# Strassen's step of the gate and up product starts one block earlier (block 4 instead of 5), with one token sum made by accumulating transfers

## The chip, the cores and the metric

The kernel runs on one core of a Trainium2 chip. The core has a matrix engine (TensorE, PE in the rows; PEld is its weight load), a vector engine (VectorE, DVE), a scalar engine (ScalarE, ACT), GpSimd (POOL) and SyncE (SP), each with its own instruction stream that it works off in order, and 16 DMA engines that the streams of SP, ACT and POOL feed. The metric is the device time of one execution in microseconds (us), lower is better. The kernel before takes 902.25 us (median of 3 runs, 900.49 to 902.29).

## The reference, cut to what matters

One decoder layer for 512 tokens of width 1024. After the token mixers comes the feed-forward part, and there the change lies:

```python
    h = rmsnorm(x, norm_ffn_pre[i])                       # 512 x 1024
    gate, up = jnp.split(h @ ffn_w_gate_up[i], 2, axis=-1)  # two products with 1024 x 2816
    x = x + rmsnorm((jax.nn.silu(gate) * up) @ ffn_w_down[i], norm_ffn_post[i])
```

All of it is float32. The change leaves the results the same up to rounding.

## The kernel before, in words

**The split.** Each operand of a product is cut into a rounded high part and a low rest (`h` by a ScalarE copy into the type fp32r, `l` by a VectorE subtraction `x - h`), and a product is three matmuls: high x high, high x low, low x high. The normed tokens lie transposed in `aTh` (high) and `aTl` (low), as 8 slices of 128 model channels by 512 tokens.

**The blocks.** Gate and up have 22 blocks each (`f` = 0 to 21) of 128 output channels. A block loads 512 KB of gate and 512 KB of up weights by SP (`raw` tiles), cuts them (`wh`, `wl`), and multiplies.

- Blocks 0 and 1 run ahead of the loop, blocks 2 to 4 in the ordinary form: 2 x 8 x 3 = 48 matmuls of 512 columns (`gu_mm`), then ScalarE's silu and VectorE's product (`gu_act`, the `L1192` and `L1193` rows).
- From `f == SF` on (SF = 5 before) a block runs in Strassen's form (`s_block`): gate and up weights are seen as a 2 x 2 block matrix (gate or up, lower or upper half of the model channels), the tokens as another (halves of the channels, halves of the tokens). Seven products of 12 matmuls of 256 columns replace eight. They use sums of weights, made anew for each block (`s_load`: `s12`, `s34`, then cut to `w12`, `w34`, and `vw`, whose low part is finished by an accumulating DMA from POOL, `L1325`), and sums of tokens T1 to T4, made once ahead of the first such block (`t_sums`).

**The token sums.** With lo1, lo2 the lower channels of the first and second half of the tokens and hi1, hi2 the upper ones, each in a high and a low part: T1 = lo1 - lo2, T3 = hi2 - lo2, T2 = T3 - lo1 up to sign, T4 = T2 - hi1 up to sign. Each elementary step is one VectorE instruction over 128 x 1024 elements; then the sum is cut (`cut`: ScalarE copy `L1268`, VectorE subtraction `L1269`). T4 is written over lo2 in `aTh` and `aTl`. Before, step 0 (T1) runs ahead of block 2, step 1 (T3) ahead of block 3, step 2 (T2, and the uncut T4) ahead of block 4, step 3 (the cut of T4) ahead of block 5.

**The order of the products in `s_block`.** gate-lower x lo1 into bank X (its sum is P1), gate-upper x hi1 into W, then `w12`-upper x T2 into X again, *on top of* P1; so this third product cannot begin before ScalarE has copied P1 out of X (`nc.scalar.copy(P1, X)`, `L1362`). Then `w12`-lower x T1, `w34`-lower x T3, `w34`-upper x hi2, `vw` x T4.

**What sets the order.** TensorE's order is the program's (`strict`). On the other engines a scheduler puts instructions in order at build time: DMAs and cuts of weights inside `tc.high_priority(offset=...)` are pulled ahead of what is written before them; the rest stays near the order of the text. A tile of a pool that is named again waits until its last reader is through.

**Weight buffers.** `s_raw` takes five buffers in turn: three of the ring `rawf`, and the two 512 KB tiles `x1_0` and `x1_1`, which come free early, as soon as two tiles of the residual are stored (`L1157`). `loads[0]` says at which of the five it starts.

Of the kernel before, what the change touches and what calls it, by code (L numbers as in the profile page):

```python
# [8 lines left out]
F32 = mybir.dt.float32  # L9
F32R = mybir.dt.float32r  # L10
BF16 = mybir.dt.bfloat16
AF = mybir.ActivationFunctionType
OP = mybir.AluOpType
# [21 lines left out]
TV = (12, 7, 8, 11)  # L35
VP = (4,)

SF = 5
SA = 160
WARM = 13  # L40

# [1 line left out]
def f32(ap):  # L43
    return ap.bitcast(F32)
# [3 lines left out]
def layer_kernel(ctx, tc, a, out):  # L48
    nc = tc.nc
# [13 lines left out]
    def nm(s):  # L63
        uid[0] += 1
        return f"{s}{uid[0]}"

    def bank(tag, shape=None):
        return ps.tile(shape or [128, 512], F32, tag=tag, name=nm(tag), bufs=PB[tag])
# [1054 lines left out]
    def gu_load(f, up=None):  # L1123
        return (wload(wgu[:, :, f * 128:(f + 1) * 128], [128, KT, 128], "f"),
                wload(wgu[:, :, DFF + f * 128:DFF + (f + 1) * 128], [128, KT, 128], "f", up))
# [41 lines left out]
    NJ2, HS = NF // 2, S // 2  # L1167
# [3 lines left out]
    def gu_mm(w, banks, cs, then=None):  # L1171
        for i, ((wh, wl), p_) in enumerate(zip(w, banks)):
            three(p_[:, cs], [(wh[:, k], wl[:, k], aTh[:, k, cs], aTl[:, k, cs]) for k in range(KT)],
                  {TK[2]: then} if i == 1 and then else {})

    def gu_act(f, pg, pu):

        j, odd = divmod(f, 2)
        b, jj = divmod(j, 2)
        if not odd:  # L1180
            ST[j] = ff.tile([128, 2, S], F32, tag="st" if j else "s10", name=nm("st"), bufs=2 if j else 1)
        st = ST[j][:, odd]
        if odd and jj == 0:
            n = len(BLK[b])
            RA[b] = dram.tile([128, n, 4, HS], F32, name=nm("rd"))
            A11[b] = ff.tile([128, n, 2, HS], F32R, tag=f"a{b}", name=nm("a"))
        r = ff.tile([128, 4, HS], F32, tag="rs", name=nm("r")) if odd else None
        o_ = r[:, 0:2].rearrange("p a q -> p (a q)") if odd else st
        if callable(pg):
            pg(st, o_)  # L1190
        else:
            last["silu"] = tab(nc.scalar.activation(st, pg, AF.Silu))  # L1192
            nc.vector.tensor_mul(o_, pu, st)  # L1193
        if not odd:
            return
        x = ST[j]
        e, s_ = x[:, 0], x[:, 1]
        ah = A11[b][:, jj]
        nc.scalar.copy(ah[:, 0], e[:, :HS])
        nc.vector.tensor_sub(ah[:, 1], e[:, :HS], f32(ah[:, 0]))  # L1200
        nc.vector.tensor_add(r[:, 3], e[:, HS:], r[:, 1])
        nc.vector.tensor_sub(s_[:, :HS], r[:, 3], e[:, :HS])
        nc.vector.tensor_sub(s_[:, HS:], e[:, :HS], e[:, HS:])
        nc.vector.tensor_sub(r[:, 2], r[:, 0], s_[:, :HS])
        nc.gpsimd.dma_start(RA[b][:, jj], r)
        s23 = ff.tile([128, 2, 2, HS], F32R, tag=f"s{j}", name=nm("s"))
        sv = s_.rearrange("p (o q) -> p o q", o=2)
        nc.scalar.copy(s23[:, :, 0], sv)
        nc.vector.tensor_sub(s23[:, :, 1], sv, f32(s23[:, :, 0]))
        S23[j] = s23  # L1210
# [33 lines left out]
    SB = {}  # L1244
    half = KT // 2
    tokens = [slice(0, HS), slice(HS, S)]

    def part_of(lo_hi, tok):
        ks = slice(half * lo_hi, half * lo_hi + half)
        return aTh[:, ks, tokens[tok]], aTl[:, ks, tokens[tok]]  # L1250

    def home(tag, shape, dt=F32R):
        return ff.tile(shape, dt, tag=tag, name=nm("T"))

    def t_sums(step):

        if step == 0:
            SB["tmp"] = [home(t_, [128, half, HS], F32) for t_ in ("s8", "s9")]
        n_ = ("T1", "T3", "T2", "T4")[step]
        SB[n_] = part_of(0, 1)  # L1260
        if step < 3:
            t_ = home(n_.lower(), [128, 2, half, HS])
            SB[n_] = t_[:, 0], t_[:, 1]
        x, z = SB["tmp"]
        lo1, lo2, hi1, hi2 = ([f32(v) for v in part_of(a_, b_)] for a_ in range(2) for b_ in range(2))

        def cut(n_, v):
            nc.scalar.copy(SB[n_][0], v)  # L1268
            nc.vector.tensor_sub(SB[n_][1], v, f32(SB[n_][0]))  # L1269

        def diff(o_, t_, p_, q_):
            nc.vector.tensor_sub(o_, p_[0], q_[0])
            nc.vector.tensor_sub(t_, p_[1], q_[1])
            nc.vector.tensor_add(o_, o_, t_)

        def minus(o_, v, q_):
            nc.vector.scalar_tensor_tensor(o_, v, -1.0, q_[0], op0=OP.mult, op1=OP.subtract)
            nc.vector.tensor_sub(o_, o_, q_[1])

        if step == 0:  # L1280
            diff(x, z, lo1, lo2)
            cut("T1", x)
        elif step == 1:
            diff(z, x, hi2, lo2)
            cut("T3", z)
        elif step == 2:
            minus(x, z, lo1)
            cut("T2", x)
            minus(z, x, hi1)
        else:  # L1290
            cut("T4", z)

    loads = [0]

    def s_raw(src):

# [9 lines left out]
    def s_load(f):  # L1306
# [21 lines left out]
        def behind(name):  # L1328

            if f == SF:  # L1330
                name = {"P5": "silu", "U3": "cut"}[name]
# [15 lines left out]
    def s_block(f):  # L1347
        gw, w12, w34, vw = s_load(f)
        X, Z, W = (bank(t_)[:, :HS] for t_ in ("mm", "sc", "tr"))
        if f == SF:  # L1350
            SB["tmp"] = home("tm", [128, half, HS], F32)
        P1, P5, U2, U3 = (SB["tmp"][:, i] for i in range(half))

        def times(p_, w, at, b, fresh=False):
            for k in range(half):
                for n_, (u, m_) in enumerate(((0, 0), (0, 1), (1, 0))):
                    mm(p_, w[u][:, at + k], b[m_][:, k], start=fresh and k == 0 and n_ == 0,
                       stop=k == half - 1 and n_ == 2, skip_group_check=not fresh)

        def act(st, o_):  # L1360
            times(X, gw, 0, part_of(0, 0), True)
            nc.scalar.copy(P1, X)  # L1362
            times(W, gw, half, part_of(1, 0), True)
            nc.vector.tensor_add(st[:, :HS], W, P1)
            times(X, w12, half, SB["T2"])
            nc.scalar.copy(U2, X)
            times(Z, w12, 0, SB["T1"], True)
            last["P5"] = nc.scalar.copy(P5, Z)
            times(X, w34, 0, SB["T3"])
            last["U3"] = nc.scalar.copy(U3, X)  # L1370
            times(Z, w34, half, part_of(1, 1))
            nc.vector.tensor_add(st[:, HS:], Z, U2)
            last["silu"] = tab(nc.scalar.activation(st, st, AF.Silu))
            times(X, vw, 0, SB["T4"])
            nc.vector.tensor_add(U3, U3, P5)
            nc.vector.scalar_tensor_tensor(o_[:, :HS], X, -1.0, st[:, :HS], op0=OP.mult, op1=OP.mult)
            last["o2"] = nc.vector.scalar_tensor_tensor(o_[:, HS:], U3, -1.0, st[:, HS:], op0=OP.mult, op1=OP.mult)

        gu_act(f, act, None)

    strict[0] = True
    for f in range(2, NF):
        if f - 2 <= SF - 2:
            t_sums(f - 2)
        if f >= SF:
            s_block(f)
            continue
        w, banks = gu_load(f), (bank("mm"), bank("sc"))
        gu_mm(w, banks, slice(0, S))
        gu_act(f, *banks)  # L1390
# [127 lines left out]
    for b, js in enumerate(BLK):  # L1518
# [4 lines left out]
        for jj, j in enumerate(js):  # L1523
            with tc.high_priority(offset=dn[0]):
                x = ff.tile([128, 2, 2, HS], F32R, tag=f"s{3 + j % 4}", name=nm("p"))
# [199 lines left out]
```

## Time and profile before

| what | value |
|---|---|
| runs before | 902.25 us median (900.49, 902.25, 902.29) |
| profiled execution | 901.4 us, span 899.6 us from the first to the last instruction, so 1.8 us around it |
| granted TensorE clock, mean over the span | 0.999 of full speed |
| busy: PE, PEld, DVE, ACT, POOL | 888.6, 763.2, 705.1, 556.7, 160.0 us |
| DMA moved | 110.94 MB |

The span is the time that the profile sees; sums below are made against 901.4 us, the time of that same execution, which lies 0.85 us under the median. An engine that is busy nearly all the time sets the end, if its work follows itself without gaps; of the others only those instructions matter for which it waits. Times of instructions are us from the start of the span.

### The profile page before, as it was taken

What the parts mean: (1) busy time and instruction counts of PE and PEld (TensorE: products, weight loads), DVE (VectorE), ACT (ScalarE), POOL (GpSimd) and SP (SyncE); (2) the same over time, 40 slices, a digit from 0 to 9 for tenths busy, and PEclk for the clock granted to TensorE, in tenths of its full rate; (3) what the DMA queues carried; (4) which work ended last, traced back from release to release, by engine and by line L of the source; (5) the groups of instructions that cost most, each with busy time, mean ns of one, the idle gap of its engine ahead of it and who ended that gap; (6) DMA issues with size and microseconds to landing.
All of it is one profiled execution on the core that took longest, in us unless ns stands there. A gap on an engine that the chain in (4) does not pass through costs nothing.

```text
span 899.6 us, 14169 instructions
## 1 busy us (share of the span) xinstructions
PE 888.6 (99%) x5105; PEld 763.2 (85%) x5105; DVE 705.1 (78%) x1366; ACT 556.7 (62%) x1072; POOL 160.0 (18%) x247
## 2 busy tenths in 40 slices
PE   8999999999999999999999999999999999999997
PEld 6977888878888888888888988999999988878886
DVE  6657786968788788787857588888888898888852
ACT  6468958667677667767735345766676653466520
POOL 4001201214143232323402100111111100002000
PEclk9999999999999999999999999999999999999999
DMA  9433335292114111111138244666566665658511
GB/s 300 95 94 100 111 97 162 72 163 64 45 45 106 48 48 48 47 48 47 36 133 254 94 129 118 165 164 153 142 175 168 168 217 181 195 179 243 174 58 47
DMA packets 138934, 110.94 MB, mean 123 GB/s; under 512 B 6936, under 2 KB 119664, under 8 KB 138864
## 3 DMA queue, kind: packets, MB, share of 16 engines
q1 hardware_dynamic: 126272, 95.61, 36.2%
q0 software_dynamic: 12576, 14.42, 8.2%
q8 instruction: 40, 0.66, 0.3%
q14 instruction: 30, 0.25, 0.1%
q10 hardware_dynamic: 16, 0.00, 0.0%
HBM read 97.96 MB, written 8.91 MB: 119 GB/s over the span
## 4 chain that ended last, share of the span: by engine, by line
PE 89%; DVE 5%; ACT 3%; DMA 2%; issue 1%; SPq 1%; POOL 0%; DVEq 0%; ACTq 0%
PE mm L100 46%; PE sc L100 19%; PE tr L100 7%; PE mq L100 7%; PE pv L100 5%; PE tr L103 4%; DVE wl L162 1%; DMA KS<-KS 1%; DMA y<-in_w_in_dram 1%; DVE e L845 1%; ACT e L848 1%; DVE PT L931 1%; ACT wh L161 1%; PE sc L103 0%; DVE r L644 0%
## 5 line engine op out<-in xcount | busy, mean ns | idle before, releaser
L100 PE MATMUL mm<-aTh,wh 128*128 128x512 f32 (+1 forms) x400 | 159.1, 398 | 0.1
L100 PE MATMUL mm<-aTl,wh 128*128 128x512 f32 (+1 forms) x400 | 153.3, 383 | 0.1
L100 PE MATMUL mm<-aTh,wl 128*128 128x512 f32 (+1 forms) x400 | 153.3, 383 | 0.0
L860 POOL TENSOR_SCALAR e<-e,sm 128x128 f32<-128x128 f32 (+3 forms) x128 | 77.3, 620 | 154.8 <-DVE sm L856 89.9
L162 DVE TENSOR_TENSOR wl<-raw,wh 128x1024 fp32r<-128x1024 f32 x59 | 73.1, 1242 | 28.2 <-ACT wh L161 23.6
L848 ACT ACTIVATE e<-e,mn 128x128 f32<-128x128 f32 (+3 forms) x128 | 71.5, 560 | 28.1 <-DVE mn L845 18.0
L100 PEld LDWEIGHTS mm<-aTh,wl 128*128 128x128 f32 x400 | 75.3, 188 | 15.1
L100 PEld LDWEIGHTS mm<-aTh,wh 128*128 128x128 f32 x400 | 75.4, 189 | 14.3 <-issue 3.4
L100 PEld LDWEIGHTS mm<-aTl,wh 128*128 128x128 f32 x400 | 75.6, 189 | 10.9 <-DVE aTl L248 0.5
L161 ACT CAST wh<-raw 128x1024 fp32r<-128x1024 f32 x59 | 61.6, 1048 | 28.5 <-PE mm L100 25.2
L845 DVE CUSTOM_DVE_ANT_0 e<-sc,toep 128x128 f32<-128x128 f32 (+3 forms) x128 | 59.7, 484 | 16.5 <-PE sc L100 15.5
L931 DVE TENSOR_TENSOR PT<-tr,PT 128x512 fp32r<-128x512 f32 x96 | 56.5, 595 | 15.3 <-ACT PT L930 14.7
L930 ACT CAST PT<-tr 128x512 fp32r<-128x512 f32 x96 | 47.8, 510 | 24.1 <-PE tr L103 23.2
L1316 DVE TENSOR_TENSOR w<-T,w 128x1024 fp32r<-128x1024 f32 x34 | 41.6, 1223 | 22.0 <-ACT w L1315 22.0
L100 PE MATMUL sc<-KS,QS 128*128 128x512 f32 (+2 forms) x192 | 54.3, 365 | 0.3 <-DMA KS<-KS 0.3
L100 PE MATMUL mm<-T,w 128*128 128x256 f32 x408 | 54.0, 282 | 0.0
L100 PE MATMUL mm<-aTh,w 128*128 128x256 f32 x272 | 51.5, 282 | 0.0
L100 PEld LDWEIGHTS mm<-T,w 128*128 128x128 f32 x408 | 50.9, 189 | 0.0
L103 PE MATMUL tr<-ident,e 128*128 128x128 f32 x320 | 48.6, 273 | 0.6 <-DVE PT L931 0.6
L103 PEld LDWEIGHTS tr<-ident,e 128*128 128x128 f32 x320 | 39.8, 140 | 9.6 <-DVE PT L931 0.8
L100 PEld LDWEIGHTS mm<-aTh,w 128*128 128x128 f32 x272 | 43.1, 189 | 0.0
L100 PE MATMUL mm<-T,aTh 128*128 128x512 f32 (+1 forms) x144 | 41.1, 371 | 0.0
(437 smaller groups left out, 2260.0 us busy)
## 6 DMA issues: line engine op xcount, KB each, us to landing
raw<-in_w_in_dram SPq DMA_DIRECT2D x48, 512.0 KB, 3.8
raw<-in_ffn_w_gate_up_dram SPq DMA_DIRECT2D x44, 512.0 KB, 4.1
raw<-in_ffn_w_down_dram SPq DMA_DIRECT2D x25, 512.0 KB, 4.4
rd<-r POOLq DMA_DIRECT2D x11, 512.0 KB, 4.1
w<-in_ffn_w_gate_up_dram POOLq DMA_DIRECT2D x17, 256.0 KB, 5.5
raw<-in_ple_w_gate_dram SPq DMA_DIRECT2D x8, 512.0 KB, 4.4
x<-in_x_dram SPq DMA_DIRECT2D x7, 512.0 KB, 7.9
raw<-in_w_out_dram SPq DMA_DIRECT2D x6, 512.0 KB
```

The lines of the kernel that those rows point to most:

```text
L100: return pe(nc.tensor.matmul(*args, **kw))
L103: return pe(nc.tensor.transpose(*args))
L161: nc.scalar.copy(h, RAW[n])
L162: nc.vector.tensor_sub(l, RAW[n], f32(h))
L845: nc.vector.tensor_tensor_reduce(e[:, br, :], src, toep[:, 384 - 128 * i:S], SLOPE[h], BIG, op0=OP.add, op1=OP.min, accum_out=mn[:, u, br: ...
L848: tt(nc.scalar.activation(e[:, br, :], e[:, br, :], AF.Exp, scale=-1.0, bias=mn[:, u, br:br + 1], accum_out=sm[:, u, br:br + 1]))
L860: nc.gpsimd.tensor_scalar(ev, ev, sm[:, v, br:br + 1], 1.0, op0=OP.mult, op1=OP.mult)
L930: nc.scalar.copy(P[:, 0, :2 * n], pt[:, :2 * n])
L931: nc.vector.tensor_sub(P[:, 1, :2 * n], pt[:, :2 * n], f32(P[:, 0, :2 * n]))
L1316: nc.vector.tensor_sub(l, x, f32(h))
```

## The change

The first Strassen block is block 4. All four steps of the token sums must be through one block earlier: step 0 ahead of block 2, steps 1 and 2 ahead of block 3, step 3 ahead of block 4. The three VectorE instructions of T3 go: ScalarE writes -lo2 (high part into `z`, low part into `w_`), and three accumulating DMAs from POOL add `w_`, hi2's high part and hi2's low part into `z`, 512 KB each, into the same bytes and so one after the other. Two more 512 KB tiles (the homes `s7` and `s6`) hold `z` and `w_`. The buffers start at the fourth of five (`loads = [3]`), so that block 4's gate and up weights go into `x1_0` and `x1_1`.

```diff
-SF = 5
+SF = 4
...
         if step == 0:
-            SB["tmp"] = [home(t_, [128, half, HS], F32) for t_ in ("s8", "s9")]
+            SB["tmp"] = [home(t_, [128, half, HS], F32) for t_ in ("s8", "s9", "s7", "s6")]
...
-        x, z = SB["tmp"]
+        x, y_, z, w_ = SB["tmp"]
...
         if step == 0:
-            diff(x, z, lo1, lo2)
+            nc.scalar.activation(z, lo2[0], AF.Copy, scale=-1.0)
+            nc.scalar.activation(w_, lo2[1], AF.Copy, scale=-1.0)
+            for v in (w_, *hi2):
+                nc.gpsimd.dma_start(z, v, accum_op=OP.add)
+            diff(x, y_, lo1, lo2)
             cut("T1", x)
         elif step == 1:
-            diff(z, x, hi2, lo2)
             cut("T3", z)
...
-    loads = [0]
+    loads = [3]
...
-        if f - 2 <= SF - 2:
-            t_sums(f - 2)
+        for step in {2: (0,), 3: (1, 2), SF: (3,)}.get(f, ()):
+            t_sums(step)
```

Lines behind `t_sums` carry numbers that are 4 higher after the change (`L1362` is now `L1366`, `L1315` `L1319`, `L1316` `L1320`, `L1325` `L1329`).

POOL, from the last rows ahead of the feed-forward loop on, in the kernel before (`xd`: the stored residual, `r` to `rd`: a block's values kept in DRAM, `w`: the low part of `vw`):

```order
L1157 DMA xd_5279<-x_5027 128x1024
L1157 DMA xd_5280<-x_5028 128x1024
L1205 DMA rd_5542<-r_5544 128x1024
L1205 DMA rd_5542<-r_5698 128x1024
L1325 DMA w_5806<-in_ffn_w_gate_up_dram 128x4x128
```

and the same place now (`T_5559` is `z`, `T_5560` is `w_`):

```order
L1157 DMA xd_5279<-x_5027 128x1024
L1157 DMA xd_5280<-x_5028 128x1024
L1285 DMA T_5559<-T_5560 128x1024
L1205 DMA rd_5542<-r_5544 128x1024
L1285 DMA T_5559<-aTh 128x4x256
L1285 DMA T_5559<-aTl 128x4x256
L1329 DMA w_5745<-in_ffn_w_gate_up_dram 128x4x128
```

The second accumulating transfer stands behind the store of `r`, which VectorE's `L1204` of blocks 0 and 1 must have finished; each waits for the landing of the one before it.

VectorE from the end of the ordinary block 2 on, now (`T_5557` is `x`: T2 uncut; `T_5637`, `T_5640` the cut T3 and T2; the `w` rows are low parts of weights; `raw_5853`, `raw_5855` are block 5's weights):

```order
L1200 TENSOR_TENSOR a_5543<-st_5634,a_5543 128x256
L1277 SCALAR_TENSOR_TENSOR T_5557<-T_5559,aTh 128x1024
L1269 TENSOR_TENSOR T_5637<-T_5559,T_5637 128x1024
L1278 TENSOR_TENSOR T_5557<-T_5557,aTl 128x1024
L1277 SCALAR_TENSOR_TENSOR T_5559<-T_5557,aTh 128x1024
L1320 TENSOR_TENSOR w_5738<-T_5733,w_5737 128x1024
L1269 TENSOR_TENSOR T_5640<-T_5557,T_5640 128x1024
L1341 TENSOR_TENSOR T_5862<-raw_5855 128x512
L1278 TENSOR_TENSOR T_5559<-T_5559,aTl 128x1024
L1320 TENSOR_TENSOR w_5750<-T_5734,w_5749 128x1024
```

The second of these rows is the first that reads `z` after the transfers; all rows behind it wait with it. Ahead of this piece the four weight sums of block 4 (128 x 512 each) now stand in front of the first token sum.

ScalarE around the copy of P1, before (block 5, P1's copy is `L1362`) and now (block 4, `L1366`):

```order
L1322 CAST w_5805<-raw_5787 128x512
L1323 ACTIVATE w_5806<-w_5805 128x512
L1268 CAST aTh<-T_5558 128x4x256
L1315 CAST w_5810<-T_5795 128x512 x2
L1199 CAST a_5820<-st_5780 128x256
L1362 COPY T_5818<-mm_5815 128x256
```

```order
L1326 CAST w_5744<-raw_5726 128x512
L1268 CAST T_5640<-T_5557 128x1024
L1327 ACTIVATE w_5745<-w_5744 128x512
L1319 CAST w_5749<-T_5734 128x512 x2
L1268 CAST aTh<-T_5559 128x4x256
L1366 COPY T_5757<-mm_5754 128x256
```

In both the high part of T4 (`aTh<-T`) is cut ahead of the copy of P1; now it stands directly ahead of it.

## Rows read from the trace of the kernel before

**Rows 1.** The page, part 1: busy us (share of the span) and instructions of each engine.

```profile
PE 888.6 (99%) x5105; PEld 763.2 (85%) x5105; DVE 705.1 (78%) x1366; ACT 556.7 (62%) x1072; POOL 160.0 (18%) x247
```

**Rows 2.** The chain that ended last, merged, blocks 3 to 6: start, us, what.

```profile
534.22 5.44 PE mm L100 x24
...
545.10 5.44 PE mm L100 x24
...
557.41 1.44 PE tr L100 x12
...
567.39 1.44 PE tr L100 x12
```

**Rows 3.** Who waited for whom on PE over the whole span, the longest: total, times, longest.

```profile
PE sc L100 <- DVE warm L374: 1.4, 1, 1.4
```

**Rows 4.** Timeline of PE, first matmuls of block 4 and of block 5's first three products.

```profile
544.93 0.39 PE L100 MATMUL mm<-aTh,wh 128*128 128x512 f32 x1
...
555.81 0.28 PE L100 MATMUL mm<-aTh,w 128*128 128x256 f32 x1
...
557.25 0.28 PE L100 MATMUL tr<-aTh,w 128*128 128x256 f32 x1
...
558.68 0.52 PE L100 MATMUL mm<-T,w 128*128 128x256 f32 x3
```

**Rows 5.** Timeline of ACT, blocks 2 to 5.

```profile
522.38 1.09 ACT L1192 ACTIVATE st<-mm 128x512 f32<-128x512 f32 x2
...
528.36 1.05 ACT L1268 CAST T<-T 128x1024 fp32r<-128x1024 f32 x1 [0.51 <-DVE T L1274]
...
553.29 1.05 ACT L1268 CAST aTh<-T 128x1024 fp32r<-128x1024 f32 x1
...
557.45 0.37 ACT L1362 COPY T<-mm 128x256 f32<-128x256 f32 x1 [0.21 <-PE mm L100]
```

**Rows 6.** Timeline of DVE, start of block 2.

```profile
521.11 1.23 DVE L89 TENSOR_TENSOR wl<-raw,wh 128x1024 fp32r<-128x1024 f32 x1 [1.66 <-ACT wh L88]
522.25 1.22 DVE L1272 TENSOR_TENSOR T<-aTh 128x1024 f32<-128x1024 f32 x1
...
525.12 0.68 DVE L1193 TENSOR_TENSOR r<-sc,st 128x512 f32<-128x512 f32 x1
525.72 0.41 DVE L1200 TENSOR_TENSOR a<-st,a 128x256 fp32r<-128x256 f32 x1
526.05 0.42 DVE L1201 TENSOR_TENSOR r<-st,r 128x256 f32<-128x256 f32 x1
```

**Rows 7.** Line L1205: plain stores of 512 KB from POOL, ns on POOL, landing.

```profile
L1205 POOL DMA_DIRECT2D rd<-r x11: 531/576/578, 528.9 to 729.5; - x11
...
DMA to landing us min/median/max: 2.9/4.1/4.4
```

**Rows 8.** Line L1325: accumulating transfers of 256 KB from DRAM, 512-byte pieces.

```profile
L1325 POOL DMA_DIRECT2D w<-in_ffn_w_gate_up_dram x17: 1264/1274/1364, 553.7 to 715.2; - x17
...
DMA to landing us min/median/max: 5.1/5.5/6.9
```

**Rows 9.** Line L1552: four accumulating transfers of 256 KB within SBUF, 2 KB pieces.

```profile
DMA to landing us min/median/max: 4.1/7.1/8.6
```

**Rows 10.** DMA queues, 553.6 to 560.5, one L1325: packets, MB, share of 16 engines.

```profile
q0 software_dynamic: 528, 0.26, 31.3%
```

**Rows 11.** DMA queues, 825 to 838, the four L1552.

```profile
q0 software_dynamic: 576, 1.05, 46.2%
```

**Rows 12.** Timeline of PE at the start: warming matmuls of 512 columns.

```profile
1.45 3.17 PE L100 MATMUL sc<-warm 128*128 128x512 bf16 x7 [1.45 <-DVE warm L374]
...
4.75 2.73 PE L100 MATMUL sc<-warm 128*128 128x512 bf16 x6
```

**Rows 13.** Windows at the end: length, busy PE PEld DVE ACT POOL, PEclk, DMA, GB/s.

```profile
894.00:895.00 1.00, 0.68 (x6) 0.47 (x4) 0.28 (x1) 0.00 (x0) 0.00 (x0) 1.00 0.38 131
...
898.00:899.00 1.00, 0.00 (x0) 0.00 (x0) 0.00 (x0) 0.00 (x0) 0.00 (x0) 0.60 0.00 0
```

## The prediction

> **What bounds the kernel now.** I read the page's busy shares first, then the chain that ended last, then TensorE's waits, and only then the timelines of the engines around block 4. TensorE is busy for 888.6 of 899.6 us [rows 1], and its longest wait in the whole span is 1.4 us, at the very start [rows 3]. So between blocks there is nothing to gain from making another engine faster; time is saved only by giving TensorE less to do, and lost wherever something it needs comes late. The reader should see in [rows 2] that the chain through this stage is TensorE alone, one block after another: an ordinary block takes 545.10 - 534.22 = 10.88 us, a Strassen block (from one `tr` product to the next) 567.39 - 557.41 = 9.98 us.
>
> **What the change removes.** One ordinary block becomes a Strassen block: 10.88 - 9.98 = 0.90 us. That is the whole gain. It is 0.1% of the run, and a measurement of this kernel can tell about 0.2% (1.8 us) from no change. The three VectorE instructions that go (1.14 us each by the distance of starts in [rows 6]) are worth nothing by themselves, since TensorE does not wait for VectorE in this stage.
>
> **What it adds to the path.** Everything block 4 needs must now be ready one block earlier. In the new order the token sum T3 comes out of a chain of three transfers, and I follow that chain.
>
> *Its start.* ScalarE's two silu copies of blocks 0 and 1 run at 522.38 and take 1.09 [rows 5]. The two negated copies come next, 128 x 1024 each; a plain copy of that size takes 1.05 [rows 5], so `w_` is ready at 522.38 + 1.09 + 2.10 = 525.6.
>
> *First transfer.* 512 KB in 4 KB pieces. A plain store of that size lands in 2.9 at the least [rows 7]; for the adding I allow 4.6 (worked out below), so 530.2. The bounds, 2.9 and 8.6, give 528.5 and 534.2.
>
> *The store behind it.* POOL's next row is `rd<-r`, and it needs VectorE's `L1204`. From the start of the third cut at 521.11, VectorE now does 1.14 for it, four weight sums at 0.60 = 2.40, one token difference 1.14, two products 1.20, four short rows at 0.33 = 1.33, another token row 1.14 (distances of starts, [rows 6]): 521.11 + 8.35 = 529.46, and `L1204`, of the same shape as `L1201`, ends 0.42 later at 529.9. POOL spends 0.58 on the store [rows 7], so the second accumulating transfer goes out at 530.45, whether the first one took 2.9 or 4.9.
>
> *Second and third transfer.* The trace has no such transfer: 512 KB, SBUF to SBUF, adding, in 512 pieces of 1 KB. The nearest row is `L1325`, also adding, also 512 pieces, but of 512 bytes: 5.1 to 6.9, median 5.5 [rows 8]. Its packets hold each of the 16 engines for 31.3% of 6.9 us = 2.16 us [rows 10]. The four transfers of 256 KB in 2 KB pieces hold them for 46.2% of 13 us, 1.50 us each [rows 11]. For 512 KB that makes 3.0 us in 2 KB pieces and 4.3 in 512-byte pieces; for 1 KB I take 3.3, which is 1.1 to 1.2 more than `L1325` holds them. So 5.5 + 1.0 = 6.5 us each. Lower bound 2.9, the fastest plain transfer of 512 KB [rows 7]; upper bound 8.6, the slowest accumulating one [rows 9]. I stay near `L1325`, because it shares the pieces' number and the POOL time (1.27 us) with the new ones. They add into the same bytes and cannot overlap: the last lands at 530.45 + 6.5 + 6.5 = 543.45.
>
> *From the landing to TensorE.* VectorE stands at the first `L1277`, the first reader of `z`: seven rows of 6.1 us in all (four of 1.14, two of 0.60, one of 0.33) lie between `L1204` and it, so it is there at about 536 to 537. From it on come, in order, six rows of 1.14 (T2's two steps, the cut of T3, T4's first step, the low part of `w12`, the cut of T2), one weight sum of 0.60 and T4's second step of 1.14: 8.58 us. Then ScalarE cuts T4 (1.05) and only then copies P1 (0.37) [rows 5]. With 0.1 for the hand-over that is 10.1 us. The third product of block 4 adds onto P1's bank, so it cannot start before that copy: 543.45 + 10.1 = 553.55.
>
> *When TensorE wants it.* Block 4 begins at 544.93, and its third product would begin 558.68 - 555.81 = 2.87 later, at 547.80 [rows 4]. The wait is 553.55 - 547.80 = 5.75 us. It covers the others: T1, T3 and the first weights are there by then, `w34` is cut 1.14 behind T4's difference and so before P1's copy, and T4's low part, five VectorE rows and some 4 us later, is wanted four products, 5.7 us, after the third one starts. Block 5's weights wait behind the same VectorE queue, but TensorE's own stall gives that back. So the wait is paid once.
>
> *What costs nothing.* The two loads into `x1_0` and `x1_1` take the place that two loads for blocks 6 and later had in SP's order, ahead of blocks 2's and 3's last loads, so they are early. The weight sums moved ahead delay the `L1193` rows of blocks 0 and 1 by 1.3 us; their bank is wanted again only half a block later. Were that cover gone, it would cost those 1.3 us.
>
> **Sum.** -0.90 + 5.75 = +4.85 us. From the profiled 901.4 that is 906.25; the median of the runs, 902.25, lies 0.85 higher, so 907.1.
>
> **A limit to keep in mind.** No wait arises if the last transfer lands by 547.80 - 10.1 = 537.7. Gain and loss cancel at 538.6 (4.1 us for each of the two transfers), and the loss passes 0.2% at 540.4 (5.0 us each). The whole question is on which side of 4.1 to 5.0 us these transfers are.
>
> **Rivals.**
>
> *The transfers land in time (not slower).* Place: the second and third transfer. If they behave like the fastest plain ones, 2.9 each [rows 7], the last lands at 530.45 + 5.8 = 536.25, before 537.7, and only the 0.90 is left: 902.25 - 0.90 = 901.35. For it speak the plain store of 512 KB and the fastest of `L1552`, 4.1 for half the bytes [rows 9]. Against it: no accumulating transfer of 512 pieces landed in under 5.1, with half the bytes [rows 8]. It decides at 4.1 us each. The Trainium skill, page "DMA: Bandwidth & Descriptors", section "Anatomy of one DMA — SWDGE (gpsimd) path", puts a transfer issued by GpSimd at about 2.0 us plus its bytes at 436 GB/s; as an estimate from that page, 512 KB take 3.2 us, the last lands at 536.85 and the time is this rival's 901.35. By that fit `L1325`'s 256 KB would land in 2.6, and [rows 8] has 5.5, so the trace does not bear it out for accumulating transfers.
>
> *TensorE's clock falls in the stall.* After its last matmul, at 894.68, TensorE idles, and its granted clock, at full speed until then, is 0.60 in 898 to 899 and so has fallen to the lower of its two levels (1.2 GHz) at about 898.2, 3.5 us after the work ended [rows 13]. The stall foretold is 5.75 us. At the start the 13 warming matmuls of 512 columns follow each other at some 0.45 us, against 10.88 / 48 = 0.227 in a block, for the 6.0 us from 1.45 to 7.48 [rows 12]. If the clock falls and takes as long to come back, half of 6.0 us is lost: 907.1 + 3.0 = 910.1. Against it: one fall, at the end of the program, is all the trace has, and the stall is not much longer. The page "TensorE: Matmul & The Clock Gate" of the Trainium skill, section "Part 1: The HAM clock gate", has the same mechanism: idling throttles the array to half its rate and activity releases it; it would give this rival's time.
>
> *The transfers are slower still.* At 8.6 each [rows 9], pushed aside by the weight loads on the same engines, the last lands at 547.65; the wait is 9.95, the time 902.25 + 9.05 = 911.3. Against it: those `L1552` ran while DMA was near saturation, which this stage is not.
>
> **How the numbers follow.** The stall at full clock has 0.45, with the clock falling 0.30, transfers in time or nearly so 0.15, much slower transfers 0.10. The forecast is the first, 907.1. From 902.5 (a wait that just outweighs the gain) to 911.5 I leave out most of the third case and a part of the last. Slower by over 0.2% are the first, second and fourth: 0.84, as a little of the first lies under 5.0 us per transfer. Within 0.2%: 0.15. Faster by over 0.2% would need twice the gain that TensorE's matmuls hold: 0.01.
>
> **What will show it.** On PE a single wait of about 6 us in block 4, between its `tr` product and the next `mm` one, released by ScalarE's `L1366`; blocks 0 to 3 and 5 to 21 as before. On VectorE a wait of about 6 us ahead of the first `L1277`, released by a transfer. On POOL `L1285` three times, landing 4 to 7 us after issue. I am wrong if the transfers land in under 4.1 us, if another row than P1's copy holds TensorE, or if the granted clock shows a dent after block 4.

## The result and the profile after

The changed kernel takes 908.89 us (median of 4 runs, 908.23 to 909.69) beside 901.77 for the kernel before on the same chip: a ratio of 1.0087, 95% interval 1.0075 to 1.0099. The forecast was 907.1 us, with 902.5 to 911.5 as its range. The profiled execution has a span of 906.4 us, 6.8 more than the one of before (899.6), and a mean granted clock of 0.996 (before: 0.999).

Part 1 of the page of the changed kernel, which answers to [rows 1]:

```profile
PE 889.4 (98%) x5141; PEld 765.2 (84%) x5141; DVE 706.9 (78%) x1372; ACT 561.5 (62%) x1084; POOL 164.3 (18%) x251
```

No engine has much more work than before; TensorE is idle for longer. Where, the waits of PE from 515 to 600 us say, in a single row (who waited for whom: total, times, longest):

```profile
PE mm L100 <- ACT T L1366: 5.6, 1, 5.6
```

[Rows 3] had 1.4 us as the longest wait of the whole span. L1366 is ScalarE's copy of P1 in block 4. The chain that ended last, followed back through this stage, shows what that copy waited for (start, us, what):

```profile
530.13 0.53 POOL rd L1205
530.65 0.01 issue
530.66 1.35 POOL T L1285
532.02 5.26 issue
...
537.30 6.00 DMA T<-aTl
543.30 0.02 issue
543.32 1.22 DVE T L1277
544.54 1.14 DVE T L1269
545.68 1.15 DVE T L1278
...
550.95 1.15 DVE T L1278
552.09 0.02 issue
552.12 0.03 ACT aTh L1268
552.14 0.93 issue
553.07 0.37 ACT T L1366
553.44 0.04 issue
553.49 2.93 PE mm L100 x12
```

In [rows 2] the chain through this stage was TensorE alone. Now, in the piece shown, it runs off TensorE for 23 us: the store `rd<-r` on POOL, the second transfer behind it (the 5.26 of "issue" are its flight), the third (6.00), VectorE's T2 and T4, ScalarE's cut of T4, P1's copy. The issues of the three transfers on POOL and their landings, from the view of line L1285:

```profile
DMA to landing us min/median/max: 4.5/6.0/6.3
```

The timeline of VectorE shows how it stood in front of the last of them (in brackets the idle time before a row, and what ended it):

```profile
536.29 0.42 DVE L1200 TENSOR_TENSOR a<-st,a 128x256 fp32r<-128x256 f32 x1
543.32 1.22 DVE L1277 SCALAR_TENSOR_TENSOR T<-T,aTh 128x1024 f32<-128x1024 f32 x1 [6.61 <-DMA T<-aTl]
```

And TensorE's third to fifth product of block 4, from its timeline:

```profile
553.49 2.93 PE L100 MATMUL mm<-T,w 128*128 128x256 f32 x12 [5.58 <-ACT T L1366]
556.22 2.37 PE L100 MATMUL sc<-T,w 128*128 128x256 f32 x12
558.43 1.60 PE L100 MATMUL mm<-T,w 128*128 128x256 f32 x12
```

By the starts, the third product takes 2.73 and the fourth 2.21, where the distance of products in [rows 4] is 1.43. The windows of one microsecond tell why (length, busy PE PEld DVE ACT POOL, PEclk, DMA, GB/s):

```profile
550.00:551.00 1.00, 0.00 (x0) 0.00 (x0) 1.00 (x3) 0.00 (x0) 0.01 (x1) 1.00 0.13 15
551.00:552.00 1.00, 0.00 (x0) 0.00 (x0) 1.00 (x1) 0.00 (x0) 0.00 (x0) 0.57 0.92 115
...
556.00:557.00 1.00, 1.00 (x6) 1.00 (x6) 1.00 (x3) 0.37 (x1) 0.00 (x0) 0.50 0.00 0
557.00:558.00 1.00, 1.00 (x7) 1.00 (x6) 1.00 (x2) 0.00 (x0) 0.00 (x0) 0.52 0.62 178
558.00:559.00 1.00, 1.00 (x10) 1.00 (x10) 0.23 (x1) 0.37 (x2) 0.00 (x0) 1.00 1.07 318
```

The granted clock drops to the lower of its two levels (0.50, 1.2 GHz) at about 551.1 and is back at about 558.0. So 2.73 + 2.21 - 2 x 1.43 = 2.1 us are lost to the clock. The books close: -0.90 (block 4 is now a Strassen block) + 5.6 (wait) + 2.1 (clock) = +6.8 us, the difference of the spans.

### The profile page after: what moved, and what is told of

It reads as the page before. It is cut to its first block, busy times and chain, and to the rows that moved or that the text cites. A ratio compares the mean times of both kernels' runs of the same rounds, so it can differ in the third digit from the quotient of the medians.

```text
span 906.4 us, 14272 instructions
## 1 busy us (share of the span) xinstructions
PE 889.4 (98%) x5141; PEld 765.2 (84%) x5141; DVE 706.9 (78%) x1372; ACT 561.5 (62%) x1084; POOL 164.3 (18%) x251
## 4 chain that ended last, share of the span: by engine, by line
PE 84%; DVE 6%; issue 4%; ACT 3%; DMA 1%; POOL 1%; SPq 1%; DVEq 0%; POOLq 0%; ACTq 0%
PE mm L100 44%; PE sc L100 17%; PE mq L100 7%; PE tr L100 6%; PE pv L100 5%; PE tr L103 4%; DVE wl L162 1%; DMA y<-in_w_in_dram 1%; DMA T<-aTl 1%; DVE aTl L1412 1%; ACT e L848 1%; DVE PT L931 0%; PE sc L103 0%; ACT wh L161 0%; DVE r L644 0%
## 5 line engine op out<-in xcount | busy, mean ns | idle before, releaser
L100 PE MATMUL mm<-aTh,wh 128*128 128x512 f32 (+1 forms) x392 | 155.8, 397 | 0.1
L100 PE MATMUL mm<-aTl,wh 128*128 128x512 f32 (+1 forms) x392 | 150.1, 383 | 0.1
L100 PE MATMUL mm<-aTh,wl 128*128 128x512 f32 (+1 forms) x392 | 150.1, 383 | 0.0
L100 PEld LDWEIGHTS mm<-aTl,wh 128*128 128x128 f32 x392 | 74.0, 189 | 10.6 <-DVE aTl L248 0.5
L100 PE MATMUL mm<-T,w 128*128 128x256 f32 x432 | 58.5, 286 | 5.6 <-ACT T L1366 5.6
L1320 DVE TENSOR_TENSOR w<-T,w 128x1024 fp32r<-128x1024 f32 x36 | 44.0, 1222 | 20.9 <-ACT w L1319 20.8
L100 PEld LDWEIGHTS mm<-T,w 128*128 128x128 f32 x432 | 55.0, 192 | 5.8 <-ACT T L1366 5.8
L100 PE MATMUL mm<-aTh,w 128*128 128x256 f32 x288 | 54.5, 282 | 0.0
L100 PEld LDWEIGHTS mm<-aTh,w 128*128 128x128 f32 x288 | 45.6, 189 | 0.0
L1329 POOL DMA_DIRECT2D w<-in_ffn_w_gate_up_dram x18 | 23.0, 1278 | 107.5 <-ACT w L1327 107.5
```

Source lines behind the costliest of these rows:

```text
L100: return pe(nc.tensor.matmul(*args, **kw))
L1320: nc.vector.tensor_sub(l, x, f32(h))
L1329: nc.gpsimd.dma_start(l, wgu[:, hi, c:c + 128], accum_op=OP.add)
```

## The experiments

Each ratio is to the kernel before, run on the same chip. "Standstill" is VectorE's idle time in front of T3's first readers (in the last kernel 1.0 of it; the other 4.1 stand in front of weight sums, for weights that have not landed), "wait" the sum of TensorE's waits in blocks 4 to 6.

| kernel | us | ratio, interval | standstill | wait |
|---|---|---|---|---|
| changed | 908.89 | 1.0087 [1.0075, 1.0099] | 6.6 | 5.6 |
| no transfers | 900.44 | 0.9996 [0.9987, 1.0005] | 0 | 0.2 |
| T3 on VectorE | 903.25 | 1.0022 [1.0012, 1.0032] | 0 | 1.8 |
| P1 ahead of T4's cut | 905.52 | 1.0050 [1.0036, 1.0064] | 6.6 | 2.4 |
| extra matmuls | 910.89 | 1.0112 [1.0096, 1.0127] | 6.6 | 3.5 |
| extra matmuls, s cut later | 906.20 | 1.0059 [1.0043, 1.0074] | 6.6 | 0.3 |
| early chain | 903.39 | 1.0031 [1.0019, 1.0042] | 3.9 | 2.2 |
| T3 on GpSimd | 900.05 | 0.9993 [0.9984, 1.0002] | 0 | 0.3 |
| one transfer more | 915.23 | 1.0159 [1.0145, 1.0173] | 12.1 | 10.6 |
| from block 5 on | 907.33 | 1.0073 [1.0060, 1.0086] | 7.5 | 4.8 |
| early chain, s cut later | 900.20 | 0.9993 [0.9984, 1.0002] | 3.4 | 0 |
| GpSimd, s cut later | 900.15 | 0.9994 [0.9985, 1.0003] | 0 | 0 |
| from block 5 on, filled | 901.11 | 1.0004 [0.9995, 1.0014] | 5.1 | 0.3 |

**Without the transfers.**

```diff
-            for v in (w_, *hi2):
-                nc.gpsimd.dma_start(z, v, accum_op=OP.add)
```

> Leaves out the three accumulating transfers, so that T3 is only the negated high part of lo2 (the values of the blocks from 4 on are not the reference's); all else as in the changed kernel. Theory A (the landing of the third transfer and the queue behind it make the whole loss): no wait of TensorE in block 4, granted clock 1.00 throughout, 0.9 us under the kernel before, so about 900.9. Rival B (starting a block earlier crowds VectorE and ScalarE, whatever makes T3): a wait of 2 us or more before the third product of block 4 stays, 903 or more. Rival D (the weight sums put ahead of the token sums, or the loads in other buffers, cost): 902 to 904 with waits elsewhere in blocks 2 to 5.

Measured: 900.44 us. The wait of 5.6 us and the dent in the clock are gone; what is left in block 4 is one small wait, in the waits of PE:

```profile
PE sc L100 <- ACT T L1370: 0.2, 1, 0.2
```

So the transfers, and not the other moves of the change, bring the loss.

**T3 on VectorE, one block earlier.** The negated copies and the transfers go, and T3 is a `diff` again.

```diff
-            nc.scalar.activation(z, lo2[0], AF.Copy, scale=-1.0)
-            nc.scalar.activation(w_, lo2[1], AF.Copy, scale=-1.0)
-            for v in (w_, *hi2):
-                nc.gpsimd.dma_start(z, v, accum_op=OP.add)
...
+            diff(z, y_, hi2, lo2)
             cut("T3", z)
```

> T3 by three VectorE instructions again, as in the kernel before, with the negated copies and the transfers gone; block 4 still the first Strassen block. Theory A: VectorE has no transfer to wait for; its rows up to the cut of T2 end at about 546.1, before TensorE wants T2 at 547.8, and the cut of T4 at about 553.7, within 0.3 us of its product: 0.6 to 0.9 us under the kernel before, about 901. Rival B: VectorE is too full for 3.4 us more, a wait of 2 to 4 us in block 4, 903 to 905. If transfers are needed to start at block 4 at all, this is slower than e1 by 2 us or more.

Measured: 903.25, and not the kernel without transfers. Block 4 runs at full pace, but block 5 waits twice, by the waits of PE:

```profile
PE mm L100 <- ACT T L1367: 1.0, 1, 1.0
PE mm L100 <- ACT T L1363: 0.8, 1, 0.8
```

L1363 is P1's copy. It overwrites block 4's P1, which VectorE's L1365 still has to read, and the timeline of ScalarE shows it waiting for that row:

```profile
558.84 0.37 ACT L1363 COPY T<-mm 128x256 f32<-128x256 f32 x1 [2.12 <-DVE st L1365]
```

Three VectorE rows of 1.14 us, 3.4 in all, cost 2.8 us here beside the kernel without transfers; 1.6 of the 2.8 show as longer waits of TensorE (1.8 against 0.2). VectorE has no 3.4 us to spare once Strassen's step begins at block 4.

**P1's copy ahead of T4's cut.** The cut of T4 (`t_sums(3)`) is handed out behind the copy of P1.

```diff
-            nc.scalar.copy(P1, X)
+            p1 = nc.scalar.copy(P1, X)
+            if f == SF:
+                with tc.issue_after(p1.ins):
+                    t_sums(3)
```

> Only the order on ScalarE differs: P1 is copied ahead of the cut of T4. Theory A: the third product then waits for T2's low part only, the sixth VectorE row behind the landing (543.3 + 6.9 = 550.2, a wait of about 2.4 us), and the last product waits some 1.2 us for T4's low part; each wait is shorter than the 3.5 us after which the clock fell at the end of the run before, so the clock stays at 1.00: -0.9 + 3.6 = 2.7 us over the kernel before, about 904.5. Rival: if something else than P1's copy holds the third product, the wait of 5.6 us stays and the time is that of the changed kernel, 908.9.

Measured: 905.52; P1's copy starts at 549.06 and the third product at 549.47, so the order on ScalarE was worth 3.7 us of the wait in front of that product (1.9 left of 5.6), with VectorE's standstill unchanged. The waits add up to 2.4 us, less than theory A's 3.6; it missed the time mainly because the clock falls here too, after an idle time of only 1.9 us, and when the third product is already running. The windows around it:

```profile
549.00:550.00 1.00, 0.38 (x1) 0.19 (x1) 1.00 (x2) 0.42 (x2) 0.70 (x1) 1.00 0.17 50
550.00:551.00 1.00, 0.90 (x7) 0.91 (x8) 1.00 (x3) 0.00 (x0) 0.00 (x0) 1.00 0.50 54
551.00:552.00 1.00, 1.00 (x8) 1.00 (x7) 1.00 (x2) 0.19 (x1) 0.00 (x0) 0.57 1.13 138
```

**TensorE kept busy in the wait.** Ahead of block 4's third product, 24 matmuls whose results nobody reads:

```diff
+            if f == SF:
+                idle = bank("pv")
+                for i in range(24):
+                    mm(idle, gw[0][:, i % KT], aTh[:, i % half + half], start=i == 0, stop=i == 23)
             times(X, w12, half, SB["T2"])
```

> 24 matmuls of 512 columns into an unused bank (5.4 us of work whose result nobody reads) stand between the second and the third product of block 4. Theory A with the clock as a term of its own: the third product starts at the same 553.5, but the granted clock stays at 1.00 and the third and fourth product take 1.43 each in place of 2.73 and 2.21: 2.1 us less than the changed kernel, about 906.8. Rival C (the clock costs nothing, or most of the loss): 908.9 unchanged, or under 904.

Measured: 910.89, slower than the changed kernel. The third and fourth product started at full clock, as expected; but on ScalarE block 3's `s` cut, which waits for VectorE, now stood ahead of U2's copy, and a new wait of 3.5 us came at the fifth product, with a fall of the clock of its own. As a test of the clock's price this is inconclusive, and it was made again with that cut handed out behind U3's copy:

```diff
-        nc.scalar.copy(s23[:, :, 0], sv)
-        nc.vector.tensor_sub(s23[:, :, 1], sv, f32(s23[:, :, 0]))
+        if f == SF - 1:
+            last["cut_s"] = cut_s
+        else:
+            cut_s()
...
+                with tc.issue_after(last["U3"].ins):
+                    last["cut_s"]()
```

> The changed kernel with 24 extra matmuls of 512 columns ahead of block 4's third product (their results are used nowhere), and with block 3's s cut handed out behind U3's copy so that it no longer stands ahead of U2's copy. Theory A (the chain of transfers is late by 5.6 us, and the clock's fall in the stall costs a further 2.1 us as a term of its own): third product at about 553.5 as in the changed kernel, third and fourth product 1.43 each, granted clock 1.00 all through 550 to 560, 908.9 - 2.1 = 906.8 us. Rival C (the third and fourth product are slow for what they read, not for the clock): they keep 2.7 and 2.2, and the time stays at 908.9.

Measured: 906.20. From the timeline of PE, the extra matmuls and the next three products:

```profile
548.06 5.63 PE L100 MATMUL pv<-aTh,w 128*128 128x512 f32 x24
553.53 1.60 PE L100 MATMUL mm<-T,w 128*128 128x256 f32 x12
554.97 1.60 PE L100 MATMUL sc<-T,w 128*128 128x256 f32 x12
556.41 1.60 PE L100 MATMUL mm<-T,w 128*128 128x256 f32 x12
```

The third product starts where it does in the changed kernel (553.53 and 553.49), at full clock, and the products follow at 1.44. The two of them win 2.1 us, the ratio 0.28% (2.5 us). The clock is a term of its own.

**The chain earlier.** The negated copies and the transfers are handed out ahead of block 2's first cuts.

```diff
+            with tc.high_priority(offset=1000):
                 nc.scalar.activation(z, lo2[0], AF.Copy, scale=-1.0)
+                last["neg"] = nc.scalar.activation(w_, lo2[1], AF.Copy, scale=-1.0)
...
+            if "neg" in last:
+                order.enter_context(tc.issue_after(last["neg"].ins))
```

> The changed kernel with the two negated copies and the three transfers handed out ahead of block 2's first ScalarE cuts, at about 510 instead of 523.3, and the three transfers ahead of the store of r on POOL. Theory A (what counts is when the last transfer lands, with a limit of 537.7): the last lands at about 512 + 4.5 + 6.5 + 6 = 529, no wait in block 4, clock 1.00, and the time is that of the kernel without transfers or better: 0.4 to 0.9 under before, about 900.3 us. Theory B (Strassen's step one block earlier overfills ScalarE and VectorE, and some wait stays wherever the transfers are): a wait of 1 us or more in blocks 4 or 5, 902 us or more.

Measured: 903.39. The last transfer lands at 531.9, 5.8 us ahead of the limit of 537.7, P1's copy is in time, and yet TensorE waits, for another copy. The timeline of ScalarE:

```profile
552.36 0.62 ACT L1210 CAST s<-st 128x512 fp32r<-128x512 f32 x1 [3.01 <-DVE st L1205]
552.88 0.37 ACT L1373 COPY T<-mm 128x256 f32<-128x256 f32 x1
```

U2's copy (L1373) stands behind block 3's `s` cut, and that one waits for a VectorE queue that is late after a standstill of 3.9 us in front of the early transfer. Theory A foretold an early landing, and had the outcome wrong; this leaves open whether VectorE is too full or only that cut is badly placed (the experiment with both edits, below, speaks for the second).

**T3 on GpSimd.** Three tensor operations take the place of the copies and the transfers.

```diff
+            nc.gpsimd.tensor_sub(z, hi2[0], lo2[0])
+            nc.gpsimd.tensor_sub(w_, hi2[1], lo2[1])
+            nc.gpsimd.tensor_add(z, z, w_)
```

> The changed kernel with T3 worked out by three GpSimd tensor operations of 128 x 1024 in place of the two negated copies and the three transfers. Theory A: at 2 to 2.6 us each T3 is ready some 8 us after its first reader may start, far ahead of 537.7, no wait in block 4: 0.4 to 0.9 under before, about 900.3 us. Theory B: as VectorE's version showed, a wait in block 5 of 1 us or more, 902 us or more. If GpSimd holds VectorE up while both work, VectorE's rows of 1.14 beside the three operations become longer, and the wait lies in block 4 or 5.

Measured: 900.05. They run back to back from 509.19 to 516.4, 2.40 us each, in the timeline of POOL:

```profile
509.19 2.40 POOL L1282 TENSOR_TENSOR T<-aTh 128x1024 f32<-128x1024 f32 x1 [3.99 <-ACT aTh L247]
```

VectorE is idle for most of that time; the one row that it starts beside them takes 2.69 us where its like takes 1.23. No standstill, and a wait of 0.3 us.

**One transfer more.** `w_` is added twice, so T3 has other values.

```diff
-            for v in (w_, *hi2):
+            for v in (w_, w_, *hi2):
```

> The changed kernel with the second negated half added twice, so four transfers in the chain instead of three (T3's values are other ones for it). Theory A: VectorE's row behind the last transfer, and P1's copy with it, come one transfer of 6 to 6.5 us later; TensorE's wait is 5.6 + 6.2 = 11.8 us, and the time 908.9 + 6.2 = 915.1 us, the clock's loss being paid once. Theory B (the wait is the VectorE and ScalarE queue's, whatever the transfers do): the wait grows by less than 2 us.

Measured: 915.23, where theory A had 915.1, but not in the way it said. P1's copy comes only 1.2 us later than in the changed kernel, since VectorE's rows stand in another order behind the landing. The rest of the standstill comes out at three other places:

```profile
PE mm L100 <- ACT T L1366: 6.9, 1, 6.9
PE mm L100 <- DVE aTl L1269: 1.8, 1, 1.8
PE mm L100 <- DVE T L1269: 0.9, 1, 0.9
PE mm L100 <- ACT T L1370: 0.9, 1, 0.9
```

Together 10.6 us for a standstill of 12.1: the lateness comes out again, but not along one path. That the time agrees is luck. The wait is 1.2 us shorter than theory A's 11.8, and the clock costs more: the span is 12.9 us longer than before, so -0.9 + 10.6 + 3.2 for the clock, where the changed kernel lost 2.1.

**Strassen's step from block 5 on.** The transfers stay, one ordinary block more lies ahead of them.

```diff
-SF = 4
+SF = 5
...
-    loads = [3]
+    loads = [0]
```

> The changed kernel with Strassen's step from the sixth block on again (block 5), so with the three transfers and the new order of the token sums, but one ordinary block of 10.9 us more ahead of them. Theory A (the loss is the lateness of the chain against block 4, and the transfers cost nothing by themselves): the last transfer lands at about 543.5 as in the changed kernel, P1's copy is wanted at about 558.7 and comes ahead of it; no wait, clock 1.00, and the time is that of the kernel before, 900.9, within 0.5 us. Rival (VectorE's pause of 6.6 us in front of the transfer delays what stands behind it, the cuts of weights and tokens, whatever the block): a wait of 1 us or more in block 4, 5 or 6, 902 us or more.

Measured: 907.33, and theory A fails. The last transfer lands at 544.3 and P1's copy is wanted at 558.9, 14.6 us later, where the changed kernel's whole path behind the landing took 10.1. TensorE still waits 4.8 us for that copy. The timeline of VectorE, and then that of ScalarE:

```profile
536.45 0.42 DVE L1200 TENSOR_TENSOR a<-st,a 128x256 fp32r<-128x256 f32 x1
544.35 1.22 DVE L1277 SCALAR_TENSOR_TENSOR T<-T,aTh 128x1024 f32<-128x1024 f32 x1 [7.48 <-DMA T<-aTl]
```

```profile
563.09 0.40 ACT L1199 CAST a<-st 128x256 fp32r<-128x256 f32 x1 [2.08 <-DVE st L1193]
563.40 0.37 ACT L1366 COPY T<-mm 128x256 f32<-128x256 f32 x1
```

P1's copy stands behind a cut (the a-cut, L1199) that waits for VectorE's row for block 4's gate, and VectorE comes to that row only at 562.37. Before, the same cut stood ahead of the same copy and cost nothing: VectorE came to that row at 556.01, and the cut began at 556.83. From the landing until then the view lists no idle time on VectorE. The windows from 545 to 568 us, of before and then of this kernel, show how little time there is to catch up:

```profile
545.00:568.00 23.00, 23.00 (x152) 21.14 (x151) 19.82 (x29) 13.72 (x26) 3.19 (x3) 1.00 0.57 152
```

```profile
545.00:568.00 23.00, 18.22 (x93) 16.11 (x92) 22.05 (x29) 11.20 (x20) 1.85 (x2) 0.88 0.40 104
```

Before, VectorE was busy for 19.82 of these 23 us, so 3.2 us were free; after a standstill of 7.5 it is busy for 22.05 and still late.

**The early chain with the s cut later.** The two edits above together: the early chain, and block 3's `s` cut behind U3's copy.

> The kernel with the early chain, and block 3's s cut on ScalarE handed out behind U3's copy of block 4 in place of ahead of U2's. Theory A (the 2.2 us that were left came because U2's copy stood on ScalarE behind a cut that waits for a queue on VectorE, and the clock fell in them): no wait for U2's copy, clock 1.00, 903.4 - 2.3 - 1.6 = about 899.5 to 900.5 us. Theory B (VectorE as such is too full one block earlier): the wait moves to another row of block 4 or 5 and 1 us or more stays, 902 us or more.

Measured: 900.20. No wait on TensorE from 490 to 620, clock 1.00; block 4 from its `tr` product to the next in the chain:

```profile
546.86 1.44 PE tr L102 x12
...
556.85 1.44 PE tr L102 x12
```

That is 9.99 us, the block's full gain. VectorE's standstill (3.4 us) is nearly that of the early chain alone (3.9), so the 2.2 us there came from the place of the `s` cut on ScalarE: theory A holds. The transfers do no harm where the standstill is short and no ScalarE copy that TensorE needs stands behind a cut that waits for VectorE.

**GpSimd with the s cut later.** The same edit on the GpSimd version.

> The kernel with T3 by three GpSimd operations, with block 3's s cut handed out behind U3's copy. Theory A: the 0.3 us of waiting in block 4 and the slow product ahead of it (0.4) go, the whole gain of 0.90 of a Strassen block is there: about 0.4 us under the same kernel without this edit, 899.8 to 900.3 us. Theory B: the s cut is late for block 3's tail and a wait of as much appears elsewhere; no difference.

Measured: 900.15, no wait and no slow product in block 4; the 0.7 us by which the span is shorter can't be told apart in the ratios (0.9994 beside 0.9993).

**From block 5 on, with the standstill filled.** T3's cut, T2 and T4 are handed out behind block 5's four weight sums and behind the cast of block 4's second weight tile. The cut of T4 moves too, from ahead of block 5's weight sums to behind its cuts of weights.

```diff
+            if f == SF:
+                with tc.issue_after(last["s34"].ins), tc.issue_after(cutw[0].ins):
+                    t_sums(1)
+                    t_sums(2)
...
+        if f == SF:
+            t_sums(3)
...
-        for step in {2: (0,), 3: (1, 2), SF: (3,)}.get(f, ()):
+        for step in {2: (0,)}.get(f, ()):
```

> The kernel with Strassen's step from block 5 on and the transfers, but T3's cut, T2 and T4 handed out behind block 5's four weight sums and behind the cut of block 4's second weight tile, so that VectorE has five rows (3.5 us) and ScalarE one cast to do in the time in which they stood still in front of the last transfer. Theory C (the loss of that kernel, 6.7 us, is VectorE's standstill of 7.5 us in a stage where it has hardly any free time, so that everything behind it in its queue comes late): most of the 3.5 us comes back, TensorE's wait of 4.8 shrinks to under 2 us, the clock does not fall, and the time is 901 to 903 us. Rival D (what is late is the chain from the last transfer through T2 and T4 to P1's copy, by its own 10 us): landing at about 544 and T4's cut at about 554 to 555 leave no wait in block 5 either way; then the wait of 4.8 must have another cause, such as the a-cut ahead of P1's copy on ScalarE, and it goes wholly, 900.9 us.

Measured: 901.11 instead of 907.33. The transfers land when they did (544.2). VectorE does its five rows in the gap, as soon as the weights have landed, in its timeline:

```profile
540.61 0.69 DVE L1343 TENSOR_TENSOR T<-raw 128x512 f32<-128x512 f32 x1 [4.09 <-DMA raw<-in_ffn_w_gate_up_dram]
...
545.27 1.22 DVE L1271 TENSOR_TENSOR T<-T,T 128x1024 fp32r<-128x1024 f32 x1 [1.03 <-ACT T L1270]
```

The wait falls from 4.8 to 0.3 us and the clock stays at 1.00. But this does not decide for theory C, since the order on ScalarE changed as well: P1's copy (here L1374) now stands ahead of the a-cut (L1201), as the timelines of VectorE and of ScalarE show:

```profile
560.38 0.68 DVE L1195 TENSOR_TENSOR st<-sc,st 128x512 f32<-128x512 f32 x1
```

```profile
557.65 0.36 ACT L1374 COPY T<-mm 128x256 f32<-128x256 f32 x1
...
561.10 0.41 ACT L1201 CAST a<-st 128x256 fp32r<-128x256 f32 x1 [1.34 <-DVE st L1195]
```

VectorE comes to the row for block 4's gate (L1195) only 2.0 us earlier than in the kernel from block 5 on, and 4.4 us later than before. Had P1's copy still stood behind the a-cut, it would have come at about 561.4 in place of 557.65, and TensorE, whose third product started at 558.53, would have waited about 3.3 us (an estimate from these rows). So about 1.5 of the 4.5 us belong to VectorE's earlier rows and about 3 to the order on ScalarE, which rival D had named; the time, 901.11, fits both theories.

## Why the prediction was right, and where it was not

**The chain.** The mechanism was right, and it held step by step. Negated copies ready: 525.6 foretold, 525.3 measured. First transfer: 4.6 and 4.5. Second one out: 530.45 and 530.66, behind the store that waits for VectorE. Second and third: 6.5 each, measured 6.3 and 6.0. Last landing: 543.45 and 543.3. From there to P1's copy: 10.1 and 10.1. Third product: 553.55 and 553.49. Wait: 5.75 and 5.6. The gain of 0.90 is there where nothing waits (9.99 us in the early chain with the later s cut, against 10.88). One part of it is luck: the 6.5 was taken from a row with the same number of pieces, and the number of pieces is at most a small part of what makes these transfers slow: with one transfer more, the second one, in 4 KB pieces, took 5.8 us.

**The mis-sized term.** The clock. The sum set it at nothing, since the case "stall at full clock" had the largest chance, and the fall (a rival, with 3.0 us) the next. It fell, and cost 2.1 us; the prediction's own list has a dent in the clock as a sign of being wrong. In the profiled executions this is the whole difference: 906.25 foretold and 908.23 measured, 2.1 for the clock less 0.15 for the shorter wait. The argument against it, that the stall was not much longer than the 3.5 us of [rows 13], was weak: the clock fell 3.2 us after TensorE went idle, well inside a stall of 5.6. The rows were there to give the fall the larger chance. The price was lower than the rival's 3.0 us since the clock came back 4.5 us after the work did (553.5 to 558.0), not 6.0. The 6.0 had been read from the spacing of the matmuls at the start [rows 12]; the windows of that stretch, 0 to 8 us, show a granted clock of 1.00, so those rows did not show how long a low clock lasts.

**"Worth nothing by themselves."** This was said of the three VectorE rows that go, and it is wrong for a step that begins at block 4: with them the time is 903.25, without them and without transfers 900.44, with T3 on GpSimd 900.05. [Rows 3], with no wait in the stage, show what VectorE holds up in the order of before; they do not show how much room it has.

**The limit of 537.7 for the landing.** It was worked out along one path, through P1's copy, and along that path it holds. As a condition for "no wait arises" it failed twice: the early chain landed at 531.9 and waited 2.2 us for U2's copy; from block 5 on, the landing had 14.6 us to P1's copy and the wait was 4.8. What the runs show in its place has two parts. VectorE works its queue off in order and is nearly full, so after a standstill everything behind it is late: from block 5 on, the row for block 4's gate came 6.4 us later than before, after a standstill of 7.5. And TensorE waits where something that it needs, mostly a ScalarE copy standing behind a cut, waits for such a late row. The standstill alone does not set the wait: 6.6 us gave 5.6, and with P1's copy ahead of T4's cut 2.4; 3.9 gave 2.2, and with the later `s` cut 3.4 gave none; the wait of 4.8 went to 0.3 while VectorE's row for the gate was still 4.4 us late. The forecast did not depend on the limit, since the chain missed it by far.

**Transfers in time.** That rival fell: no accumulating transfer of 512 KB landed in under 4.5 us here. The Trainium skill's page "DMA: Bandwidth & Descriptors", section "Anatomy of one DMA — SWDGE (gpsimd) path", whose fit gives 3.2 us as an estimate, is not borne out by these accumulating transfers (4.5, 6.3 and 6.0).

**A version without the loss.** Three of the kernels above avoid it: the early chain with the later cut, and T3 on GpSimd with or without that cut. Each lies 0.06 to 0.07% under the kernel before, with intervals that hold 1.0. That they beat it is not shown; more than 0.9 us was not to be had.

**What stays open.** Why the s cut lands ahead of U2's copy in some orders and not in others was not followed up. The split of the 4.5 us in the last experiment is an estimate; no run changed only VectorE's order or only ScalarE's there. What makes the second and third transfer slower than the first was not taken apart either.

## What to carry to other kernels

An engine's queue that runs in order pays for a late input with everything behind it. So compare the length of the standstill with the engine's free time in that stage, not only the path from the landing to the next consumer; and look on the other engines for rows that the bottleneck needs and that stand behind a row waiting for that queue. Here a new place for one such row took 2.2 to 3.7 us off the wait, without a faster transfer. Each stall of TensorE of 1.9 us or more in these runs had a second price, since the clock fell with it; put that into the sum. Removing work from an engine that nobody waits for can still be worth most of its length (here 2.8 of 3.4 us) if the same change moves the deadlines forward.

## What the runs showed of the hardware

**The clock can fall when work has already resumed.** In the six runs with a wait of 1.9 us or more in blocks 4 or 5 the granted clock went to 0.50, 2.0 to 4.1 us after TensorE went idle; in two of them (P1 ahead of T4's cut, idle for 1.9 us, and the early chain, 2.2) the matmuls were already running again. It stayed low for 3.4 us in these two, for 6.8 in the changed kernel, the first one with extra matmuls and the one from block 5 on, for 10.2 with one transfer more. In the runs whose longest wait was 1.0 us or less it did not fall. The Trainium skill's page "TensorE: Matmul & The Clock Gate", section "Part 1: The HAM clock gate", has idling throttle the array to half its rate; the 0.50 agrees.

**What the transfers took.** The first transfer, in 4 KB pieces, landed in 4.5 us, the next two, in 1 KB pieces, in 6.3 and 6.0. The piece is at most a small part of what tells them apart: with one transfer more, the second one was again in 4 KB pieces, and it landed in 5.8 us. From 525.6 to 530.2 the first had the engines to itself (the hardware queue took 0.1% of them); the second shared them with the store `rd<-r`, and during the third the weight loads took 44.4%. So the slower ones had company on the engines; no run separates that from their place in the chain.

**GpSimd beside VectorE.** A GpSimd operation of 128 x 1024 took 2.40 us, about twice VectorE's 1.23, and a VectorE row that ran beside one took 2.69.
